# A hybrid decoder step: the first stage in a fixed order on TensorE, VectorE and ScalarE

## The chip, the cores and the metric

The kernel runs on one core of a Trainium2 chip. The core has five engines, each with its own instruction sequence: TensorE (matmuls, in the profile PE, its weight loads PEld), VectorE (DVE), ScalarE (ACT), GpSimd (POOL) and SyncE (SP), which here issues the DMAs. The metric is the device time of one execution in microseconds (us).

## What is computed

The reference is one inference step of a decoder with two layers, for a prompt of 1024 tokens and 8 sample tokens, width 1024. Layer A is a gated delta-rule layer, layer B a sliding-window attention. Only the very beginning of layer A matters here:

```
def gdn_layer(x, conv_buf, s0, norm_g, w_in, conv_w, a_log, dt_bias, o_norm, w_out):
    proj = rmsnorm(x, norm_g) @ w_in
    qkv, gate, a, beta_logit = jnp.split(proj, [CONV_CH, CONV_CH + GDN_V_W, CONV_CH + GDN_V_W + GDN_HEADS], axis=-1)
    qkv, new_buf = causal_conv_silu(qkv, conv_buf, conv_w)
    ...
```

`rmsnorm` divides each token's row by the root of its mean square and multiplies it by a gain. `w_in` has the columns of q, k and v for eight heads of 128, a gate, and 16 columns for a and beta. The q, k and v columns then go through a convolution of four taps along the tokens.

## The kernel before

The 1032 tokens are nine tiles of x: eight of 128 tokens (x0 to x7) and one of 8 sample tokens (x8). They are transposed into three groups of 384, 384 and 264 tokens (`xg[0..2]`), x0 to x2 in the first, x3 to x5 in the second, x6 to x8 in the third. Each group holds a high part, rounded to the format that TensorE reads at full rate, and a low part, the rest.

*One x tile* (loop at L296 to L311). ScalarE squares the row and sums it (L301). VectorE takes the inverse root by nine small operations that each need the one before (`rsqrt`, L121 to L133), and scales the tile by it and by the gain (L304). TensorE transposes it in two halves, four blocks each, into a PSUM buffer (L308, tile name `xps`); ScalarE casts a half into the high part (L310), VectorE subtracts that from PSUM for the low part (L311). The PSUM pool `gen` has two buffers, so a half can be transposed only when the low part of the half before last is done.

*The projections.* `first_proj(gi)` (L279) does three things for one group: the a/b projection of 16 matmuls (tile `psab`), which ScalarE copies into `abT` (L285), and one projection of 24 matmuls each for the k and the q columns of head 0 (tile `pj`), whose results ScalarE copies into the convolution's input `ue` (L215 to L218). The PSUM pool `pj` has two buffers too. The weights come through `load_w`: two DMAs into raw buffers, of which there are two, ScalarE's cast to the high part (L80), VectorE's subtraction to the low part (L81). After the loop over the tiles come the three groups (L320), then the gate projection of head 0 (L323), and a block with raised priority that turns `abT` into decay factors (from L327, tiles `pst`, `psg`, `pss`).

*The taps.* At tile number `CT` = 5 TensorE also transposes the convolution's weights and stored rows (L317, tile `cps`), 24 small transposes, into `cvT`.

*The order of the work.* The first stage is written in the order above, but a scheduler in the compiler decides the order on each engine: an instruction that is ready may go ahead of others that wait. Buffers of one pool are handed out in the order of the program. DMAs are issued on SP in the order of `LO` = "0g12k345q678": x0, the gain, x1, x2, the k weights, x3 to x5, the q weights, x6 to x8, and behind them the a/b weights (L268) and the taps (L274). The nine x tiles share eight buffers. The stage that follows (L542 in the profile) has an order written out by a planner in the kernel, which keeps to it on all engines.

Of the kernel before, what the change touches and what calls it, by code (L numbers as in the profile page):

```python
# [23 lines left out]
NT = 8  # L24
# [32 lines left out]
def hybrid_step(  # L57
# [77 lines left out]
    def rsqrt(*a, **k):  # L135
        for _ in rsq(V, *a, **k):
            pass
# [65 lines left out]

    ues = []

    def conv_open(m):
        ue = uep.tile([P, 1060], F32, tag="ue", name="ue")
        G.memset(ue[:, 0:3], 0.0)
        G.tensor_copy(svw(ue)[:, :, 0:3], cvT[:, m, 0:24].rearrange("p (b i) -> p b i", i=3))
        return ue  # L210

    def conv_evac(ue, m, gi, ps):
        g0, gn = GRP[gi]
# [17 lines left out]
    with tc.tile_pool(name="p2a", reuse_waits="tile", bufs=1) as p2a, \  # L231
# [27 lines left out]
        ws0 = []  # L259
        for o in LO:  # L260
            if o == "g":
                DMA.dma_start(out=gbc, in_=norm_a[0:1, :].broadcast_to([P, D]))
            elif o in "kq":
                ws0.append(load_w(H * P if o == "k" else 0, w_in_a[0]))
            else:
                load_x(int(o))
        wab = p2a.tile([P, KT, 16], F32, name="wab")
        DMA.dma_start(out=wab, in_=w_in_a[0, :, 4096:4112].rearrange("(k p) c -> p k c", p=P))  # L268
        wabp = p2a.tile([P, KT, P], F32R, name="wabp")
        V.tensor_scalar_mul(wabp, ones.unsqueeze(1).broadcast_to([P, KT, P]), 0.0)  # L270
        V.tensor_copy(wabp[:, :, 0:16], wab)
        V.tensor_tensor(out=wabp[:, :, 32:48], in0=wab, in1=wabp[:, :, 0:16].bitcast(F32), op=ALU.subtract)
        cvr = p2a.tile([28, 3072], F32, name="cvr")
        DMA.dma_start(out=cvr[0:24], in_=state_conv[0].rearrange("b i c -> (b i) c"))  # L274
        DMA.dma_start(out=cvr[24:28], in_=conv_w_a[0])
        sel = p2a.tile([64, 16], F32, name="sel")
        V.tensor_tensor(out=sel, in0=ident[:64, 0:16], in1=ident[:64, 32:48], op=ALU.add)
        abT = p2a.tile([64, T], F32, name="abT")

        def first_proj(gi):  # L280
# [5 lines left out]
            for j, w in enumerate(ws0):  # L286
                m = (1 - j) * H
                if gi == 0:
                    ues.append((0, m, 1 - j, conv_open(m)))
                ps = pj.tile([P, 512], F32, tag="pj", name="pj")  # L290
                for _ in proj_group(*w, xg[gi], gn, ps):
                    pass
                conv_evac(ues[j][3], m, gi, ps)

        for t in range(NT + 1):
            n = P if t < NT else NS  # L296
            g, off = divmod(t * P, 384)
            xt = xts[t]
            junk = p1.tile([P, D], BF16, tag="junk", name="junk", bufs=1)
            r = sm.tile([P, 1], F32, tag="r1", name="r1")  # L300
            S.activation(junk[:n], xt[:n], AF.Square, accum_out=r[:n])  # L301
            ri = sm.tile([P, 1], F32, tag="ss", name="ri")
            rsqrt(ri[:n], r[:n], 1, 1.0 / D, EPS, n, tag="b")
            V.scalar_tensor_tensor(out=xt[:n], in0=xt[:n], scalar=ri[:n], in1=gbc[:n], op0=ALU.mult, op1=ALU.mult)  # L304
            for hf in range(2):
                ps = gps("xps").rearrange("p (k t) -> p k t", k=4)
                for k in range(4):
                    PE.transpose(ps[:, k, :n], xt[:n, ts(4 * hf + k, P)], ident[:n, :n])  # L308
                hi = xg[g][:, 0, 4 * hf:4 * hf + 4, off:off + n]
                S.copy(hi, ps[:, :, :n])  # L310
                V.tensor_tensor(out=xg[g][:, 1, 4 * hf:4 * hf + 4, off:off + n], in0=ps[:, :, :n],  # L311
                                in1=hi.bitcast(F32), op=ALU.subtract)
            if t == CT:
                for q in range(2):
                    ps = gps("cps")
                    for j in range(12):
                        PE.transpose(ps[:, j * 28:j * 28 + 28], cvr[:, ts(12 * q + j, P)], ident[:28, :28])  # L317
                    S.copy(cvT[:, 12 * q:12 * q + 12, :].rearrange("p a b -> p (a b)"), ps[:, :12 * 28])
                V.tensor_scalar_mul(cvT[:, :, 24:28], cvT[:, :, 24:28], 0.5)
        for gi in range(3):  # L320
            first_proj(gi)
        hd[0]["og"] = ogs[:, 0]
        wz = load_w(3 * H * P, w_in_a[0])  # L323
        for gi in range(3):
# [1537 lines left out]
```

## Time and profile before

| | |
|---|---|
| runs | 1304.68, 1306.94, 1301.55 us, median 1304.68 |
| profiled execution | 1303.65 us, its span 1302.0 us |
| TensorE busy | 1227.2 us, 94% |
| VectorE, ScalarE, GpSimd busy | 71%, 49%, 22% |
| mean granted TensorE clock | 0.986 of 2.4 GHz |
| chain that ended last | TensorE 70%, VectorE 17%, ScalarE 4%, DMA 4% |

The span runs from the first to the last instruction of the program. An engine is busy while one of its instructions executes; matmuls are pipelined, so that the time of one row in the timeline is longer than the distance to the next. Times in the trace count from the span's start. A granted clock of 0.50 is 1.2 GHz, 1.00 is 2.4 GHz.

### The profile page before, as it was taken

How to read it: one execution, taken by the hardware profiler on the slowest of the kernel's cores; microseconds unless marked ns; L12 is line 12 of the kernel's file. 1: busy time of each engine (PE TensorE's matmuls, PEld its weight loads, DVE VectorE, ACT ScalarE, POOL GpSimd, SP SyncE). 2: the span in 40 equal slices, each digit the busy share in tenths (PEclk: the TensorE clock that was granted, in tenths of full speed). 3: DMA queues.
4: the chain of work that ended last, by engine and by line, in shares of the span. 5: the costliest groups of instructions: out<-in, count | busy, mean ns of one | idle time of the engine just before them, and what ended most of it. 6: DMA issues, size and time to landing. Idle time of an engine off the chain costs nothing.

```text
span 1302.0 us, 24333 instructions
## 1 busy us (share of the span) xinstructions
PE 1227.2 (94%) x8887; PEld 1112.0 (85%) x8887; DVE 926.3 (71%) x2656; ACT 634.8 (49%) x1812; POOL 288.4 (22%) x404
## 2 busy tenths in 40 slices
PE   4999999999999999998999978999989999999998
PEld 3989898989999989888988746888878888988897
DVE  7468988878979897788877358686675677677221
ACT  5236555645455553546453137375565556567100
POOL 1036423424324353253301122120030020000000
PEclk9999999999999999999999989999999999999999
DMA  7021111110221322111256666121030030102322
GB/s 239 1 81 35 36 33 36 37 51 18 68 66 35 98 67 84 36 36 31 61 176 195 200 220 176 34 59 26 1 82 3 1 82 20 33 2 88 117 91 73
DMA packets 131987, 92.03 MB, mean 71 GB/s; under 512 B 33880, under 2 KB 123712, under 8 KB 131808
## 3 DMA queue, kind: packets, MB, share of 16 engines
q1 hardware_dynamic: 131868, 90.48, 23.6%
q8 instruction: 70, 1.15, 0.4%
q14 instruction: 49, 0.40, 0.1%
HBM read 69.28 MB, written 23.25 MB: 71 GB/s over the span
## 4 chain that ended last, share of the span: by engine, by line
PE 70%; DVE 17%; ACT 4%; DMA 4%; issue 3%; POOL 2%; SPq 0%; DVEq 0%; ACTq 0%; POOLq 0%
PE pj L542 24%; PE pj L99 17%; PE ivt L542 4%; DVE co L542 3%; PE sps L99 3%; PE chB L542 3%; PE op L99 2%; PE chA L542 2%; PE ptp L1645 1%; DMA out_dram<-hx 1%; DVE wqkv L81 1%; PE sp L542 1%; PE nps L542 1%; PE tq L1592 1%; PE psab L99 1%
## 5 line engine op out<-in xcount | busy, mean ns | idle before, releaser
L542 PE MATMUL pj<-xg,whi 128*128 128x384 f32 (+1 forms) x1392 | 289.9, 335 | 1.0 <-ACT whi L542 1.0
L542 PEld LDWEIGHTS pj<-xg,whi 128*128 128x128 f32 x1392 | 222.6, 190 | 2.7 <-ACT whi L542 1.2
L99 PE MATMUL pj<-wqkv,ng 128*128 128x384 f32 x768 | 154.6, 346 | 0.0
L542 PE MATMUL pj<-xg,wlo 128*128 128x384 f32 (+1 forms) x696 | 151.9, 335 | 0.0
L542 DVE SCALAR_TENSOR_TENSOR co<-ue,cvT,co 128x528 f32<-128x528 f32 x144 | 134.6, 941 | 16.1 <-ACT co L542 14.5
L99 PEld LDWEIGHTS pj<-wqkv,ng 128*128 128x128 f32 x768 | 133.2, 191 | 5.0 <-issue 4.6
L542 PEld LDWEIGHTS pj<-xg,wlo 128*128 128x128 f32 x696 | 111.8, 189 | 1.4 <-issue 0.7
L92 POOL TENSOR_TENSOR raw<-raw,gains 128x512 f32<-128x512 f32 x40 | 45.8, 1154 | 255.5 <-DMA raw<-in_w_in_b_dram 147.1
L99 PE MATMUL pj<-wob,oh 128*128 128x384 f32 (+1 forms) x576 | 98.1, 325 | 0.0
L99 PEld LDWEIGHTS pj<-wob,oh 128*128 128x128 f32 x576 | 90.7, 191 | 1.8 <-issue 1.5
L542 PE MATMUL pj<-woa,ohl 128*128 128x512 f32 x288 | 76.1, 406 | 0.0
L542 PEld LDWEIGHTS pj<-woa,ohl 128*128 128x128 f32 x288 | 51.7, 188 | 11.6 <-issue 1.5
L542 ACT COPY ue<-pj 128x384 f32<-128x384 f32 (+1 forms) x88 | 31.7, 377 | 53.1 <-PE pj L542 46.1
L1823 DVE TENSOR_TENSOR hx<-hx,pj 128x384 f32<-128x384 f32 (+3 forms) x27 | 13.7, 508 | 60.5 <-PE pj L99 45.9
L542 POOL TENSOR_TENSOR ue<-ue,co 128x528 f32<-128x528 f32 x24 | 33.9, 1412 | 71.1 <-ACT ue L542 71.1
L542 DVE TENSOR_TENSOR wlo<-raw,whi 128x512 fp32r<-128x512 f32 x58 | 43.6, 758 | 7.7 <-ACT whi L542 7.6
L542 ACT ACTIVATE ue<-co 128x528 f32<-128x528 f32 x48 | 30.8, 644 | 29.9 <-DVE co L542 27.7
L542 ACT CAST whi<-raw 128x512 fp32r<-128x512 f32 x58 | 35.8, 619 | 16.8 <-PE pj L542 16.5
L542 POOL TENSOR_TENSOR co<-co,ue 128x528 f32<-128x528 f32 x24 | 39.3, 1636 | 1.3
L99 PE MATMUL op<-pt,vsb 128*64 128x256 f32 x240 | 37.9, 396 | 0.9 <-DVE e L1629 0.8
L1536 ACT ACTIVATE jk<-pj 128x320 f32<-128x320 f32 x32 | 13.9, 435 | 50.4 <-PE pj L99 50.4
L99 PE MATMUL pj<-woa,ohl 128*128 128x512 f32 x96 | 27.7, 442 | 11.2 <-DVE ohl L1420 5.8
(906 smaller groups left out, 2965.9 us busy)
## 6 DMA issues: line engine op xcount, KB each, us to landing
raw<-in_w_in_a_dram SPq DMA_DIRECT2D x64, 256.0 KB
ssm<-in_state_ssm_dram SPq DMA_DIRECT2D x32, 256.0 KB
hD<-hx SPq DMA_DIRECT2D x16, 512.0 KB
raw<-in_w_in_b_dram SPq DMA_DIRECT2D x32, 256.0 KB
xt<-in_x_prompt_dram SPq DMA_DIRECT2D x8, 512.0 KB
out_dram<-ssm SPq DMA_DIRECT2D x16, 256.0 KB
raw<-in_w_out_a_dram SPq DMA_DIRECT2D x16, 256.0 KB
hx<-in_x_prompt_dram SPq DMA_DIRECT2D x8, 512.0 KB
```

Source lines behind the costliest of these rows:

```text
L81: V.tensor_tensor(out=lo, in0=raw, in1=hi.bitcast(F32), op=ALU.subtract)
L92: G.tensor_tensor(out=raw, in0=raw, in1=gain[:, k:k + n].unsqueeze(2).broadcast_to([P, n, c]), op=ALU.mult)
L99: PE.matmul(out, lhsT, rhs, start=start, stop=stop, skip_group_check=True)
L542: op.f(*op.a, **op.k)
L1536: S.activation(jk[:n], src, AF.Square)
L1592: PE.transpose(tq[:, ts(h, P)], qhl[:, h].rearrange("p a d -> p (a d)"), identr)
L1645: PE.transpose(pp[:, ts(h, P)], pr[h // 2][:, h % 2, ts(kt, P)], ident)
L1823: V.tensor_tensor(out=hx[:n, :cn], in0=hx[:n, :cn], in1=ps[:n, :cn], op=ALU.add)
```

## The change

The work of the tiles, from x0 to the second group's first convolution projection, is now written in one block in which TensorE, VectorE and ScalarE keep the written order (`manual_schedule`). The steps of a tile become functions: `square`, `scale`, `turn` (the transposes and both parts, a half at a time). `norm_group` squares two or three tiles, takes their inverse roots in one chain of nine operations on up to three columns, and scales them. `first_proj` is split into `first_ab` and `first_conv`; `weave` lets the next half of a tile be transposed after every four matmuls of a projection (the taps after every ten). SP's order becomes "0g12ak345678q": the a/b weights stand behind x2, the k weights come as one DMA into a buffer of their own, the q weights are loaded inside the block (`second_w`), the taps after the first convolution projection. The convolution inputs are opened (`conv_open`, on GpSimd) at the end. `turn_taps` does what L315 to L319 did. Everything from the gate projection on is as before.

```diff
-LO = "0g12k345q678"
-CT = 5
+LO = "0g12ak345678q"
...
+        wk_raw = p1.tile([P, KT, P], F32, name="wk_raw")
+        wk = [whl.tile([P, KT, P], F32R, tag=f"w{a}", name=f"w{a}") for a in ("hi", "lo")]
+        ws0 = [wk]
...
+            elif o == "a":
+                DMA.dma_start(out=wab, in_=w_in_a[0, :, 4096:4112].rearrange("(k p) c -> p k c", p=P))
+            elif o == "k":
+                DMA.dma_start(out=wk_raw, in_=w_in_a[0][:, H * P:H * P + P].rearrange("(k p) c -> p k c", p=P))
+            elif o != "q":
                 load_x(int(o))
...
+        def turn(t):
+            n = P if t < NT else NS
+            g, off = divmod(t * P, 384)
+            for hf in range(2):
+                ps = gps("xps").rearrange("p (k t) -> p k t", k=4)
+                for k in range(4):
+                    PE.transpose(ps[:, k, :n], xts[t][:n, ts(4 * hf + k, P)], ident[:n, :n])
+                hi = xg[g][:, 0, 4 * hf:4 * hf + 4, off:off + n]
+                S.copy(hi, ps[:, :, :n])
+                V.tensor_tensor(out=xg[g][:, 1, 4 * hf:4 * hf + 4, off:off + n], in0=ps[:, :, :n],
+                                in1=hi.bitcast(F32), op=ALU.subtract)
+                yield
+
+        def norm_group(tiles):
+
+            n_ = len(tiles)
+            r = sm.tile([P, 3], F32, tag="r1", name="r1")
+            if NT in tiles:
+                V.memset(r, 1.0)
+            ri = sm.tile([P, 3], F32, tag="ss", name="ri")
+            for i, t in enumerate(tiles):
+                square(t, r[:, i:i + 1])
+            rsqrt(ri[:, :n_], r[:, :n_], n_, 1.0 / D, EPS, tag="b")
+            for i, t in enumerate(tiles):
+                scale(t, ri[:, i:i + 1])
...
+        def first_conv(gi, j):
+            if gi == 0:
+                ues.append((0, (1 - j) * H, 1 - j, uep.tile([P, 1060], F32, tag="ue", name="ue")))
+            ps = pj.tile([P, 512], F32, tag="pj", name="pj")
+            yield from proj_group(*ws0[j], xg[gi], GRP[gi][1], ps)
+            conv_evac(ues[j][3], (1 - j) * H, gi, ps)
+
+        def weave(a_, b_, n):
+
+            for i, _ in enumerate(a_):
+                if i % n == n - 1:
+                    next(b_, None)
+            for _ in b_:
+                pass
...
+        def second_w():
+            ws0.append(load_w(0, w_in_a[0]))
+            yield
...
+        with tc.manual_schedule(engines={mybir.EngineType.PE, mybir.EngineType.DVE, mybir.EngineType.Activation}):
+            norm_group([0])
+            r = sm.tile([P, 3], F32, tag="r1", name="r1")
+            for i in range(2):
+                square(1 + i, r[:, i:i + 1])
+            for _ in turns([0]):
+                pass
+            ri = sm.tile([P, 3], F32, tag="ss", name="ri")
+            rsqrt(ri[:, :2], r[:, :2], 2, 1.0 / D, EPS, tag="b")
+            for i in range(2):
+                scale(1 + i, ri[:, i:i + 1])
+            V.tensor_copy(wabp[:, :, 0:16], wab)
+            V.tensor_tensor(out=wabp[:, :, 32:48], in0=wab, in1=wabp[:, :, 0:16].bitcast(F32), op=ALU.subtract)
+            for _ in turns([1, 2]):
+                pass
+            for a in range(2):
+                split(wk[0][:, ts(a, 4)], wk[1][:, ts(a, 4)], wk_raw[:, ts(a, 4)])
+            norm_group([3, 4, 5])
+            first_ab(0)
+            weave(first_conv(0, 0), seq(turns([3, 4]), second_w(), turns([5])), 4)
+            DMA.dma_start(out=cvr[0:24], in_=state_conv[0].rearrange("b i c -> (b i) c"))
+            DMA.dma_start(out=cvr[24:28], in_=conv_w_a[0])
+            norm_group([6, 7, 8])
+            weave(first_conv(0, 1), turns([6, 7, 8]), 4)
+            first_ab(1)
+            weave(first_conv(1, 0), turn_taps(), 10)
+        for _ in first_conv(1, 1):
+            pass
+        first_ab(2)
+        for j in range(2):
+            for _ in first_conv(2, j):
+                pass
+        for j in range(2):
+            conv_open(ues[j][3], ues[j][1])
         hd[0]["og"] = ogs[:, 0]
         wz = load_w(3 * H * P, w_in_a[0])
```

## Rows read from the trace of the kernel before

**Rows 1.** The page, part 1: busy us of TensorE, share, instructions.

```profile
PE 1227.2 (94%) x8887; PEld 1112.0 (85%) x8887; DVE 926.3 (71%) x2656; ACT 634.8 (49%) x1812; POOL 288.4 (22%) x404
```

**Rows 2.** Busy time of each engine by stretch, up to the next stage.

```profile
core 0: us, PE busy (x) PEld busy (x) DVE busy (x) ACT busy (x) POOL busy (x), PEclk, DMA share, GB/s
0.00:27.00 27.00, 7.47 (x33) 6.33 (x33) 19.24 (x83) 16.34 (x29) 4.46 (x19) 1.00 0.85 254
27.00:47.00 20.00, 20.00 (x134) 18.79 (x132) 14.90 (x46) 8.47 (x19) 0.34 (x2) 1.00 0.12 47
47.00:81.40 34.40, 34.27 (x224) 33.11 (x223) 10.61 (x45) 7.33 (x19) 0.25 (x1) 1.00 0.15 47
```

**Rows 3.** Who TensorE waited for, 0 to 100 us.

```profile
PE xps L308 <- DVE xt L304: 13.5, 2, 11.2
PE xps L308 <- DVE xg L311: 6.0, 2, 3.8
PE dps L542 <- POOL gm L542: 1.3, 1, 1.3
PE pj L542 <- ACT whi L542: 1.0, 1, 1.0
```

**Rows 4.** Timeline (start us, us, engine, line, operation), x0: square, root's first step, scaling.

```profile
6.90 1.06 ACT L301 ACTIVATE junk<-xt 128x1024 bf16<-128x1024 f32 x1 [2.83 <-DMA xt<-in_x_prompt_dram]
...
8.08 0.15 DVE L121 TENSOR_SCALAR rs_x<-r 128x1 f32<-128x1 f32 x1 [2.64 <-ACT junk L301]
...
9.81 1.28 DVE L304 SCALAR_TENSOR_TENSOR xt<-xt,ri,gbc 128x1024 f32<-128x1024 f32 x1
```

**Rows 5.** Timeline, ScalarE and VectorE: x2's square, casts, low parts.

```profile
11.37 1.06 ACT L301 ACTIVATE junk<-xt 128x1024 bf16<-128x1024 f32 x1 [0.16 <-DMA xt<-in_x_prompt_dram]
...
12.43 0.60 ACT L80 CAST whi<-raw 128x512 fp32r<-128x512 f32 x1
...
12.94 0.57 ACT L310 CAST xg<-xps 128x512 fp32r<-128x512 f32 x1
...
20.45 1.28 DVE L311 TENSOR_TENSOR xg<-xps,xg 128x512 fp32r<-128x512 f32 x2
```

**Rows 6.** Timeline, TensorE: the first matmuls of the a/b projection.

```profile
27.00 4.10 PE L99 MATMUL psab<-xg,wabp 128*128 128x384 f32 x12
```

**Rows 7.** Chain that ended last, 36 to 52 us: start us, us, what.

```profile
37.97 1.60 PE cps L317 x24
...
40.82 2.12 PE pj L99 x12
42.94 0.44 PE xps L308 x4
...
46.65 0.77 PE pst L99 x6
47.42 3.01 PE psab L99 x16
```

**Rows 8.** Timeline, VectorE: two steps of interleaved roots.

```profile
23.57 0.15 DVE L132 SCALAR_TENSOR_TENSOR rs_u<-rs_u 128x1 f32<-128x1 f32 x1
23.63 0.15 DVE L128 TENSOR_TENSOR rs_u<-rs_u,ri 128x1 f32<-128x1 f32 x1
```

**Rows 9.** Timeline, VectorE: second operation on the a/b weights.

```profile
26.39 0.28 DVE L272 TENSOR_TENSOR wabp<-wab,wabp 128x128 fp32r<-128x128 f32 x1
```

**Rows 10.** Timeline, ScalarE: the first a/b result leaves PSUM.

```profile
32.72 0.47 ACT L285 COPY abT<-psab 64x384 f32<-64x384 f32 x1
```

**Rows 11.** Two waits elsewhere, and the granted clock (PEclk) behind them.

```profile
486.79 0.66 PE L542 MATMUL ktp<-ident,ktok 128*128 128x128 f32 x4 [2.18 <-DVE ktok L542]
757.12 3.78 PE L99 MATMUL pj<-woa,ohl 128*128 128x512 f32 x8 [5.78 <-DVE ohl L1420]
...
488.30:491.60 3.30, 3.30 (x15) 3.30 (x14) 3.09 (x10) 1.57 (x4) 0.82 (x2) 0.50 0.00 0
757.10:760.90 3.80, 3.78 (x8) 2.48 (x8) 0.30 (x1) 0.00 (x0) 3.51 (x5) 0.50 0.95 276
```

More of the change, by code (lines that the diff above doesn't have):

```diff
@@ L204, in hybrid_step, with conv_open @@
     ues = []
-    def conv_open(m):
-        ue = uep.tile([P, 1060], F32, tag="ue", name="ue")
+    def conv_open(ue, m):
         G.memset(ue[:, 0:3], 0.0)
         G.tensor_copy(svw(ue)[:, :, 0:3], cvT[:, m, 0:24].rearrange("p (b i) -> p b i", i=3))
-        return ue
     def conv_evac(ue, m, gi, ps):
@@ L257, in load_x @@
             xts.append(xt)
-        ws0 = []
+        wab = p2a.tile([P, KT, 16], F32, name="wab")
+        wk_raw = p1.tile([P, KT, P], F32, name="wk_raw")
+        wk = [whl.tile([P, KT, P], F32R, tag=f"w{a}", name=f"w{a}") for a in ("hi", "lo")]
+        ws0 = [wk]
+        wabp = p2a.tile([P, KT, P], F32R, name="wabp")
+        V.tensor_scalar_mul(wabp, ones.unsqueeze(1).broadcast_to([P, KT, P]), 0.0)
+        sel = p2a.tile([64, 16], F32, name="sel")
+        V.tensor_tensor(out=sel, in0=ident[:64, 0:16], in1=ident[:64, 32:48], op=ALU.add)
         for o in LO:
@@ L275, in hybrid_step, with square, scale @@
-        DMA.dma_start(out=cvr[24:28], in_=conv_w_a[0])
-        sel = p2a.tile([64, 16], F32, name="sel")
-        V.tensor_tensor(out=sel, in0=ident[:64, 0:16], in1=ident[:64, 32:48], op=ALU.add)
         abT = p2a.tile([64, T], F32, name="abT")
-        def first_proj(gi):
+        def square(t, r):
+            n = P if t < NT else NS
+            junk = p1.tile([P, D], BF16, tag="junk", name="junk", bufs=1)
+            S.activation(junk[:n], xts[t][:n], AF.Square, accum_out=r[:n])
+        def scale(t, ri):
+            n = P if t < NT else NS
+            xt = xts[t]
+            V.scalar_tensor_tensor(out=xt[:n], in0=xt[:n], scalar=ri[:n], in1=gbc[:n], op0=ALU.mult, op1=ALU.mult)
@@ new lines, in turn @@
+        def turn(t):
+            n = P if t < NT else NS
+            g, off = divmod(t * P, 384)
[8 more added lines that the diff above has]
+                yield
@@ new lines, in norm_group, with turns @@
+        def norm_group(tiles):
[9 more added lines that the diff above has]
+                scale(t, ri[:, i:i + 1])
+        def turns(tiles):
+            for t in tiles:
+                yield from turn(t)
@@ L281, in first_proj, with first_ab @@
+        def first_ab(gi):
             g0, gn = GRP[gi]
@@ L285, in first_proj @@
             S.copy(abT[:, g0:g0 + gn], ps[:64, :gn])
[L286 to L319, printed above, removed]
@@ L320, in hybrid_step @@
-        for gi in range(3):
-            first_proj(gi)
+        def first_conv(gi, j):
[10 more added lines that the diff above has]
+                pass
@@ new lines, in turn_taps @@
+        def turn_taps():
+            for q in range(2):
+                ps = gps("cps")
+                for j in range(12):
+                    PE.transpose(ps[:, j * 28:j * 28 + 28], cvr[:, ts(12 * q + j, P)], ident[:28, :28])
+                S.copy(cvT[:, 12 * q:12 * q + 12, :].rearrange("p a b -> p (a b)"), ps[:, :12 * 28])
+                yield
+            V.tensor_scalar_mul(cvT[:, :, 24:28], cvT[:, :, 24:28], 0.5)
+        def second_w():
+            ws0.append(load_w(0, w_in_a[0]))
+            yield
@@ new lines, in seq @@
+        def seq(*gs):
+            for g_ in gs:
+                yield from g_
+        with tc.manual_schedule(engines={mybir.EngineType.PE, mybir.EngineType.DVE, mybir.EngineType.Activation}):
[24 more added lines that the diff above has]
+            weave(first_conv(1, 0), turn_taps(), 10)
```

10 lines of the change are left out of this document (removed).

## The prediction

> **What bounds the kernel now.** I read the page first: TensorE is busy 94% of the span [rows 1], so time is won or lost where it stands idle. The busy times by stretch say where: 7.5 us of work in the first 27 us, then 20.0 of 20.0 and 34.3 of 34.4 up to the next stage at 81.4 [rows 2]. The waits of TensorE name what it stood for in those 27 us: 13.5 us for VectorE's scaled x tiles, 6.0 us for VectorE's low parts, which free the two PSUM buffers of the transposes [rows 3]. So the first stage is a load and VectorE problem up to 27 us, and a pure TensorE problem after it. A change of order here can win at most what lies ahead of 27 us. It can also lose, by any wait that it puts after 27 us, because nothing there is slack.
>
> **The change, part by part.** I follow the new order instruction by instruction, on the time axis of the trace of before. One engine takes its instructions in the order in which the code now writes them.
>
> *Prices.* A squared row costs ScalarE 1.06 us [rows 4]. One inverse root is a chain of nine dependent VectorE operations, from 8.08 to 9.81: 1.75 us with its start. The scaling takes 1.28 us, 1.21 to the next one [rows 4]. ScalarE's casts follow each other by 0.5 us, 0.6 us long; VectorE's low parts by 0.61 us, 0.68 long [rows 5]. Four transposes take 0.44 us and a 384-column matmul 0.177 at the higher clock level; at the lower one, at which the first twelve matmuls ran, 0.34 each (the clock column reads 1.00 there; twice the spacing says 1.2 GHz), 0.32 from start to start [rows 6, 7].
>
> *Batched inverse roots.* Nine chains of nine become four. This looks like 45 operations saved, but in before the chains of different tiles are interleaved: operations of two chains start 0.06 us apart [rows 8], where those of one chain start 0.19 apart (1.75 by nine). Eight interleaved chains of nine at 0.06 and the lone first one (1.75) are 6.1 us of VectorE; four serial chains are 7.0. So nothing is won by the count; the steps below take each new chain at its 1.75. The Trainium skill ("VectorE: DVE Perf Modes", "The DRAIN you can't avoid" and "Rules for kernel authors") says that the next operation does not issue until the pipe is empty, so that only the count matters; by it 45 times 0.19, or 8.6 us of VectorE, would be saved. The trace does not agree: 0.06 us between starts of operations 0.15 us long.
>
> *Start of the first projection.* Loads of x0, the gain, x1 and x2 keep their places, so x2 is still there at 11.4 [rows 5]. Its square ends at 12.4; the casts of x0 at 13.3 to 13.9; x0's second low part frees VectorE at 14.5; roots of x1 and x2 to 16.2; x1 is scaled at 17.5, x2 at 18.7; the two operations on the a/b weights, the longer 0.28 [rows 9], take it to 19.3. The transposes, still at the lower level (0.23 each: 7.47 us for 33 in [rows 2]), the cast and the low part of x1's first half end at 20.0 and free a buffer for x2, whose second cast lands at 22.7. The a/b projection starts at 22.0 instead of 27.0: 5.0 us won. Eight transposes of x3, which before did ahead of 27, are still to come (0.9 lost), and all 16 matmuls may run at the lower level, where 11 did (0.7 lost).
>
> *The second group.* ScalarE has behind that cast two casts of the k weight (to 23.65), then the squares of x3 to x5 (3.2, to 26.9). VectorE's root takes 1.75 (28.7), the first scaling 1.28: x3's transposes start at 30.1. TensorE has finished the a/b projection (16 x 0.32 from 22.0: 27.1) and the four matmuls written ahead of them (27.9): 2.2 us of new waiting. From there to x5's last transposes 20 matmuls (3.5), 24 transposes (2.6), six changes between matmuls and transposes (an estimated 0.1 each, 0.6) and one wait of 0.5, since x3's low part, which frees the buffer for x4, is now behind the scalings of x4 and x5: TensorE is at 37.5.
>
> *The third group* decides. The squares of x6 to x8 are written after everything of the first convolution projection, so ScalarE reaches them only behind x5's last cast, at 38.3. Three squares: 41.5. Roots: 43.3. First scaling: 44.6. Transposes of x6: 44.8. TensorE has only four matmuls (37.5 to 38.2) before them in its own order: 6.6 us of waiting. In before it was never idle here [rows 2]. Behind the waiting transposes stand 20 matmuls, the a/b projection and all that follows; nothing may pass. Even later projections left to the scheduler can't, for the PSUM ring is served in program order: before had the a/b result at 33.2, but its high-priority pst took its turn in the other ring at 46.65, after the last transposes [rows 7, 10]. From 44.8: 20 matmuls 3.5, 24 transposes 2.4 (x8's are short), changes 0.6, a wait of 0.5, 16 matmuls 2.8: the second a/b projection ends at 54.5.
>
> *Comparison.* In before it ends at 50.4 with the tap transposes (1.60) and the first pst group (0.77) already done [rows 7]; without these, 48.1. New minus old: 6.5 us. As a sum: -5.0 + 0.9 + 0.7 + 2.2 + 0.5 + 6.6 + 0.5 = 6.4.
>
> *The clock.* Some 1.5 us after a wait of 2.2 us elsewhere in this kernel TensorE ran 3.3 us at granted 0.50, the level of 1.2 GHz; after one of 5.8 us it came back at 0.50 and did 3.8 us of work at it [rows 11]. After the new waits I take 3.4 us at half rate in the second group (0.6 on the path, the rest lies under VectorE) and 4 us in the third (1.4): 2.0 us. Below, nothing; above, about 4.5 if the third group stays low to its end.
>
> *Loads.* On SP's queue the a/b weights and one whole transfer of the k weights now stand ahead of x3; x3 to x7 no longer stand behind the q weights' raw buffers; only x8 still waits, for x0's buffer, free at 13. At the 254 GB/s of [rows 2] x3 (1.1 MB behind x2) is in by 16, x5 by 20, x7 by 24; the squares ask for them at 23.7, 25.8 and 39.3. I cost the loads at nothing: ScalarE's order covers them by 6 us or more. Were ScalarE ready for x3 right behind x2's square, at 12.4, x3 would be 3.4 us late.
>
> *After the fixed part* the code is as before, and TensorE has 34.3 us of work in 34.4 [rows 2]: what is late at its start is late at its end, and the next stage hangs on that.
>
> Sum: 6.5 + 2.0 = 8.5 us on the profiled execution's 1303.65 (span 1302.0 and 1.65 around it): 1312.2. The median of the runs, 1304.68, is 1.0 above that execution. I predict 1312.
>
> **Rivals.**
> *Not slower: the long wait does not arise.* Place: ScalarE and VectorE between x5's last cast and x6's scaling. If the squares of x6 to x8 are run ahead (x6 is loaded by 24) and their roots and scalings slip under the first convolution projection, the third group loses its 6.6 and its share of the clock, and the sum is -5.0 + 0.9 + 0.7, or -3.4, if the other new waits go with it, and -3.4 + 3.2 + 0.6 = 0.4 if they stay: 1300 to 1304. For it: such work was hidden in before, where VectorE had 5 us free of 20 from 27 on [rows 2]. Against it: the code order, which I take as binding. It decides whether x6's transposes start within about 2 us of the fourth matmul.
> *Partly swallowed later.* At the start of the next stage TensorE waits 1.0 us for a weight cast and 1.3 for a decay [rows 3]; if VectorE got ahead there, and no clock were lost, the sum would be 6.5 - 2.3, 1308. Against: both hang on the end of this stage.
> *The clock stays low.* Between waits the third group is a sparse mix, and the a/b projection after it may also run at 0.50: 54.5 becomes 57.4 to 58.8, that is 1315 to 1318. The skill ("TensorE: Matmul & The Clock Gate", "HAM oscillation") has an array re-throttled by each round's wait, with every round starting cold, which is this case; [rows 11] show it after two waits.
>
> **How the numbers follow.** Forecast 0.58, its own range 1308 to 1316; not slower 0.18; swallowed 0.10; clock 0.10; something unseen 0.04. A measurement tells about 0.5%, 6.5 us, from no change: slower means above 1311.2. Of the forecast 0.40 lies above it and 0.18 below, plus the clock's 0.10 and 0.02 unseen: slower 0.52. Same: 0.18 + 0.10 and 0.13 of the not-slower case: 0.41. Faster needs more than any term here gives (of the 19.5 us idle in [rows 2], 11.2 pass before x0 is scaled [rows 3]): 0.07. The range runs from inside the not-slower case to the top of the clock's: 1300 to 1318.
>
> **What would show it.** In the new profile: the first a/b matmul near 22; x3's transposes near 30, x6's near 45 with an idle time of 5 to 7 us ahead of them, released by the scaling; VectorE and ScalarE in single file in front of it; granted clock at 0.50 after it; the second a/b projection ending near 55 to 57. I am wrong if no wait of TensorE after 30 is over 2 us, or if the stage ends as early as before despite it.

## The result and the profile after

The changed kernel is slower: median 1316.55 us (1311.15 to 1319.87) against 1301.55 us (1297.54 to 1306.94) of the kernel before on the same chip, seven runs each. The ratio is 1.0105, with a 95% interval of 1.0082 to 1.0128; that is 13.7 us, between 10.7 and 16.7. The profiled execution took 1319.66 us, its span 1318.0.

The busy times by stretch of the changed kernel, cut as in [rows 2], with a fourth stretch up to the start of the next stage, which is now at 95.4 us and was at 82.5:

```profile
0.00:27.00 27.00, 9.96 (x44) 8.53 (x44) 14.71 (x44) 12.49 (x21) 4.46 (x19) 1.00 0.82 269
27.00:47.00 20.00, 8.61 (x49) 8.15 (x50) 13.48 (x32) 8.88 (x18) 0.00 (x0) 0.83 0.23 79
47.00:81.40 34.40, 32.98 (x223) 30.95 (x222) 13.81 (x51) 9.85 (x25) 0.57 (x3) 0.95 0.01 1
81.40:95.40 14.00, 13.06 (x72) 12.84 (x72) 2.73 (x5) 2.28 (x6) 0.00 (x0) 0.89 0.14 39
```

TensorE does 2.5 us more in the first 27 us (9.96 for 7.47) and then stands idle for 11.4 of 20.0 us, where in [rows 2] it was never idle. The waits of TensorE up to 100 us, as in [rows 3], name the cause: VectorE's low parts have all but gone from the list (6.0 us before, 0.5 now), and the scaled tiles cost 27.9 us for 13.5.

```profile
PE xps L292 <- DVE xt L284: 27.9, 4, 11.3
PE pj L609 <- ACT whi L609: 1.0, 1, 1.0
PE psg L98 <- DVE gf L435: 0.9, 1, 0.9
PE xps L292 <- DVE xg L295: 0.5, 1, 0.5
PE pj L98 <- ACT whi L79: 0.5, 1, 0.5
```

The timeline of the changed kernel (start us, us, engine, line, operation, in brackets the idle time ahead and what ended it), TensorE first and then what ScalarE and VectorE do in the long wait:

```profile
21.98 3.59 PE L98 MATMUL psab<-xg,wabp 128*128 128x384 f32 x16
25.40 0.86 PE L98 MATMUL pj<-xg,whi 128*128 128x384 f32 x4
30.48 1.09 PE L292 MATMUL xps<-ident,xt 128*128 128x128 f32 x4 [4.21 <-DVE xt L284]
...
37.93 0.95 PE L98 MATMUL pj<-xg,whi 128*128 128x384 f32 x4
46.80 1.08 PE L292 MATMUL xps<-ident,xt 128*128 128x128 f32 x4 [7.92 <-DVE xt L284]
...
54.76 3.09 PE L98 MATMUL psab<-xg,wabp 128*128 128x384 f32 x16
57.68 1.58 PE L98 MATMUL pj<-xg,whi 128*128 128x384 f32 x8
...
38.25 0.49 ACT L212 COPY ue<-pj 128x384 f32<-128x384 f32 x1
38.62 0.60 ACT L294 CAST xg<-xps 128x512 fp32r<-128x512 f32 x1
40.05 1.06 ACT L279 ACTIVATE junk<-xt 128x1024 bf16<-128x1024 f32 x1 [0.82 <-ACT xg L294]
...
39.90 0.06 DVE L304 MEMSET r<- 128x3 f32 x1
43.59 0.17 DVE L120 TENSOR_SCALAR rs_x<-r 128x3 f32<-128x3 f32 x1 [3.62 <-ACT junk L279]
```

The first a/b projection starts at 21.98. x3's transposes come after 4.21 us of waiting, x6's after 7.92. In front of x6's everything is in single file: x5's last cast at 38.62, the memset of the sums at 39.90 behind x5's last low part, the first square at 40.05, the roots at 43.59. The second a/b projection is over at 57.7; before, without taps and `pst`, that point was at 48.1 [rows 7]. So 9.6 us of the delay stand there.

Another 3.4 us come up to the next stage. They sit at the gate projection of head 0, in code that the change did not touch. First the kernel before, then the changed one, timelines around the cast of the gate weights and the next stage's first matmuls (L542, L609):

```profile
65.98 1.15 ACT L80 CAST whi<-raw 128x512 fp32r<-128x512 f32 x2
...
69.77 0.51 PE L99 MATMUL pj<-xg,wlo 128*128 128x384 f32 x2
70.41 0.41 PE L99 MATMUL psg<-gf,mle 128*128 128x64 f32 x2
...
82.47 1.68 PE L542 MATMUL pj<-xg,whi 128*128 128x384 f32 x8 [0.99 <-ACT whi L542]
```

```profile
80.44 0.33 ACT L447 ACTIVATE eG<-psg 128x192 f32<-128x192 f32 x1 [1.05 <-PE psg L98]
80.66 1.13 ACT L79 CAST whi<-raw 128x512 fp32r<-128x512 f32 x2
...
79.55 0.41 PE L98 MATMUL psg<-gf,mle 128*128 128x64 f32 x2 [0.91 <-DVE gf L435]
81.33 2.93 PE L98 MATMUL pj<-xg,whi 128*128 128x384 f32 x8 [0.51 <-ACT whi L79]
95.44 1.68 PE L609 MATMUL pj<-xg,whi 128*128 128x384 f32 x8 [0.99 <-ACT whi L609]
```

Before, ScalarE cast the gate weights ahead of the decay factors, and the gate's first matmuls filled the time in which the decay was worked out. Now the cast stands behind `eG`, so TensorE waits for the decay (0.91) and then for the cast (0.51), and the eight matmuls behind that run at half clock (2.93 us for eight; granted 0.50 from 81.1 to 84.6). From the next stage on the matched matmuls of the two traces stay 12.1 to 13.0 us apart up to 540 us; what is added later (17 us at the end of these two traces) comes with falls of the granted clock, which lie differently in each execution. The 13.0 us at the start of the next stage and the 13.7 us of the ratio agree.

### The profile page after: what moved, and what is told of

It is laid out like the page before. It is cut to its first block, busy times and chain, and to the rows that moved or that the text cites. A ratio compares the mean times of both kernels' runs of the same rounds, so it can differ in the third digit from the quotient of the medians.

```text
span 1318.0 us, 24284 instructions
## 1 busy us (share of the span) xinstructions
PE 1234.9 (94%) x8887; PEld 1118.3 (85%) x8887; DVE 925.3 (70%) x2612; ACT 634.6 (48%) x1812; POOL 286.6 (22%) x404
## 3 DMA queue, kind: packets, MB, share of 16 engines
q1 hardware_dynamic: 131852, 90.48, 23.1%
## 4 chain that ended last, share of the span: by engine, by line
PE 68%; DVE 18%; ACT 4%; issue 3%; DMA 2%; POOL 2%; SPq 0%; DVEq 0%; ACTq 0%; POOLq 0%
PE pj L609 23%; PE pj L98 17%; PE ivt L609 4%; DVE co L609 3%; PE sps L98 3%; PE chB L609 3%; PE op L98 2%; PE chA L609 2%; PE ptp L1712 1%; DVE wqkv L80 1%; DMA out_dram<-hx 1%; PE tq L1659 1%; PE sp L609 1%; DVE f L609 1%; DVE fu L609 1%
## 5 line engine op out<-in xcount | busy, mean ns | idle before, releaser
L609 PE MATMUL pj<-xg,whi 128*128 128x384 f32 (+1 forms) x1392 | 289.3, 335 | 1.0 <-ACT whi L609 1.0
L609 PEld LDWEIGHTS pj<-xg,whi 128*128 128x128 f32 x1392 | 222.0, 190 | 2.7 <-ACT whi L609 1.2
L609 PE MATMUL pj<-xg,wlo 128*128 128x384 f32 (+1 forms) x696 | 153.0, 336 | 0.0
L609 DVE SCALAR_TENSOR_TENSOR co<-ue,cvT,co 128x528 f32<-128x528 f32 x144 | 134.2, 938 | 7.4 <-ACT co L609 5.8
L609 PEld LDWEIGHTS pj<-xg,wlo 128*128 128x128 f32 x696 | 112.8, 191 | 1.4 <-issue 0.7
L609 PE MATMUL pj<-woa,ohl 128*128 128x512 f32 x288 | 76.1, 406 | 0.0
L609 PEld LDWEIGHTS pj<-woa,ohl 128*128 128x128 f32 x288 | 51.8, 188 | 11.5 <-issue 1.5
L609 ACT COPY ue<-pj 128x384 f32<-128x384 f32 (+1 forms) x88 | 31.7, 377 | 52.8 <-PE pj L609 45.8
L1890 DVE TENSOR_TENSOR hx<-hx,pj 128x384 f32<-128x384 f32 (+3 forms) x27 | 13.7, 508 | 59.3 <-PE pj L98 47.7
L609 POOL TENSOR_TENSOR ue<-ue,co 128x528 f32<-128x528 f32 x24 | 33.9, 1411 | 72.3 <-ACT ue L609 72.3
L609 DVE TENSOR_TENSOR wlo<-raw,whi 128x512 fp32r<-128x512 f32 x58 | 43.6, 757 | 7.7 <-ACT whi L609 7.6
L609 ACT ACTIVATE ue<-co 128x528 f32<-128x528 f32 x48 | 30.8, 644 | 29.8 <-DVE co L609 27.6
L609 ACT CAST whi<-raw 128x512 fp32r<-128x512 f32 x58 | 35.8, 619 | 17.0 <-PE pj L609 16.5
L292 PE MATMUL xps<-ident,xt 128*128 128x128 f32 (+1 forms) x72 | 14.3, 348 | 28.4 <-DVE xt L284 27.9
L609 POOL TENSOR_TENSOR co<-co,ue 128x528 f32<-128x528 f32 x24 | 38.9, 1622 | 1.3
```

Of the source, the lines that this page charges most:

```text
L292: PE.transpose(ps[:, k, :n], xts[t][:n, ts(4 * hf + k, P)], ident[:n, :n])
L609: op.f(*op.a, **op.k)
L1890: V.tensor_tensor(out=hx[:n, :cn], in0=hx[:n, :cn], in1=ps[:n, :cn], op=ALU.add)
```

## The experiments

The ratios are to the kernel before, timed on the same chip each time. Two times of the first stage say more than the medians: the second a/b projection and the start of the next stage (82.47 before, 95.44 after).

**The scheduler decides again.** Only the fixed order goes.

```diff
-        with tc.manual_schedule(engines={mybir.EngineType.PE, mybir.EngineType.DVE, mybir.EngineType.Activation}):
+        with ExitStack():
```

> The changed kernel without the fixed order: the scheduler again chooses the order of TensorE, VectorE and ScalarE; the loads, the grouped inverse roots and the weaving in the program text stay. Changed kernel now: TensorE idle 4.2 us ahead of x3's transposes and 7.9 us ahead of x6's, first matmul of the next stage at 95.4 (before: 82.5). Order theory (the written order puts the squares of x6 to x8 behind everything of the first convolution projection, and that makes the waits and the low clock): no wait of TensorE over 2 us after 30 us, gate weights cast before the gate's matmuls need them, next stage at 80 to 84, time 12 to 16 us below the changed kernel's, within 0.3% of before. Rival (grouped roots, one k transfer and the woven text cost by themselves): next stage at 90 or later, time at most 5 us below the changed kernel's.

Measured: 1298.9 us, ratio 0.9959 (0.9943 to 0.9975). All waits of TensorE from 27 us on, and the next stage's first matmul:

```profile
PE dps L609 <- POOL gm L609: 1.5, 2, 1.3
PE pj L609 <- ACT whi L609: 1.0, 1, 1.0
...
79.57 1.68 PE L609 MATMUL pj<-xg,whi 128*128 128x384 f32 x8 [0.98 <-ACT whi L609]
```

Both long waits are gone, and so is the delay ahead of the next stage; the next stage is 15.9 us earlier than in the changed kernel and 2.9 earlier than before. The time is 0.4% below before, a little more than expected. So the loss is the written order, and none of it is in grouped roots, loads or woven text.

**A fixed order for x0 to x2 only.** The block ends ahead of the squares of x3 to x5.

```diff
+        with ExitStack():
             norm_group([3, 4, 5])
             first_ab(0)
```

> The changed kernel, whose fixed order ends behind the k weights' low parts: x0 to x2 in the written order, everything from the squares of x3 on is left to the scheduler. Theory (the harm lies in the order written for the second and third group and in what it does to the gate weights' place; that of the first group costs nothing): first a/b matmul at 22.0, no wait of TensorE over 1.5 us between 27 us and the next stage, which starts at 78.5 to 82 for 95.4, time 12 to 17 us below the changed kernel. Rival (a fixed order for the first group alone already makes the stage late): next stage at 85 or later.

Measured: 1298.41 us, ratio 0.9970 (0.9941 to 0.9999); first a/b matmul at 22.10, no wait over 1.4 us from 27 us on, next stage at 78.73.

```profile
78.73 1.68 PE L610 MATMUL pj<-xg,whi 128*128 128x384 f32 x8 [0.99 <-ACT whi L610]
```

A fixed order does no harm where it is written for the first group.

**Another fixed order.** Squares of x3 to x5 in ScalarE's idle time ahead of 19 us, grouped roots cut up between low parts, each scaling just ahead of its tile's transposes. The squares of x6 to x8 come ahead too, and the gate weights have a buffer of their own, as in the run on them below; the lines shown have neither.

```diff
+            for i in range(3):
+                square(3 + i, r3[:, i:i + 1])
...
+            for n, _ in zip((1, 3, 1, 4), turns([1, 2])):
+                steps(g3, n)
+            scale(3, ri3[:, 0:1])
...
+                for _ in turn(4):
+                    steps(g6, 2)
+                    yield
...
+                scale(6, ri6[:, 0:1])
```

> A fixed order again, but another one: the squares of x3 to x5 in ScalarE's idle time between 14 and 19 us, those of x6 to x8 behind the k weights' casts and between the casts of x3 and x4, the grouped roots cut up and put between low parts, each scaling just ahead of its tile's transposes; gate weights as in e6. Order theory: first a/b projection at 22 to 23.5, no idle time of TensorE over 2 us from 27 us to the next stage, which starts at 79 to 84; time 1298 to 1305, that is 11 to 18 us below the changed kernel. Rival (a fixed order by itself, or the grouped roots, costs): next stage at 88 or later.

Measured: 1298.13 us, ratio 0.9977 (0.9956 to 0.9998). One wait over 2 us was left, 3.0 us ahead of x6's transposes at 38.16, and the next stage starts at 81.33. The expectation was none over 2 us. So it is not fixing that costs, but this order; mine is no better than the scheduler's.

**Squares of x6 to x8 ahead, two forms.** In the first the memset of their sums stands behind the scalings of x3 to x5 on VectorE.

```diff
             norm_group([3, 4, 5])
+            r678 = sm.tile([P, 3], F32, tag="r1", name="r678")
+            V.memset(r678, 1.0)
+            for i in range(3):
+                square(6 + i, r678[:, i:i + 1])
...
-            norm_group([6, 7, 8])
+            ri6 = sm.tile([P, 3], F32, tag="ss", name="ri")
+            rsqrt(ri6, r678, 3, 1.0 / D, EPS, tag="b")
+            for i in range(3):
+                scale(6 + i, ri6[:, i:i + 1])
```

> Fixed order kept; only the three squares of x6 to x8, with the memset of their sums, are written ahead, behind those of x3 to x5. Roots, scalings and transposes stay where they are. Order theory: x6's transposes start 3.5 to 4.3 us earlier than in the changed kernel (46.8), at 42.5 to 43.3, the idle time ahead of them falls from 7.9 to about 4, the next stage starts 3.5 to 6 us earlier than 95.4 (the upper end if the clock stays high), the time is 3 to 6 us lower. Rival (the wait is set by the loads of x6 to x8, or the next stage by something other than this wait): x6's transposes or the next stage move by less than 1 us.

Measured: 1316.93 us, ratio 1.0102 (1.0076 to 1.0129), nothing won; the next stage starts at 98.16, 2.7 us later than in the changed kernel. Its timeline:

```profile
32.65 0.06 DVE L374 MEMSET r<- 128x3 f32 x1
32.79 1.06 ACT L279 ACTIVATE junk<-xt 128x1024 bf16<-128x1024 f32 x1 [5.58 <-issue]
37.91 1.11 PE L292 MATMUL xps<-ident,xt 128*128 128x128 f32 x4 [3.60 <-DVE xg L295]
49.52 0.63 PE L292 MATMUL xps<-ident,xt 128*128 128x128 f32 x4 [4.20 <-DVE xt L284]
```

The memset of 0.06 us ran at 32.65, behind three scalings; the squares waited 5.58 us for it, and x3's casts behind the squares, so a new wait of 3.60 us ahead of x4's transposes took what the one ahead of x6 gave back (4.20 for 7.92). This was my edit, not the load: in the next run the same squares ran at 27.2 to 30.5 without a wait. The Trainium skill ("Perfetto Trace Analysis", "Tensor Engine Instruction (MATMUL, LD_WEIGHTS)") calls ScalarE, VectorE and GpSimd strict FIFO; this row shows what that costs.

The second form writes the memset ahead of the roots of x3 to x5.

> As the run with the squares of x6 to x8 ahead, whose squares stood 5.6 us behind a memset that VectorE reached only after the scalings of x3 to x5; here that memset is written ahead of the roots of x3 to x5. Order theory: squares of x6 to x8 end near 30.7, no new wait ahead of x4's transposes, x6's roots follow x5's last low part (about 39.9), so x6's transposes start at 42.5 to 43.5 with about 4 us idle ahead of them (changed kernel: 46.8 and 7.9), next stage 3 to 6 us earlier than 95.4, time 2 to 6 us lower. Rival (the wait of TensorE only moves, as it did in that run): sum of TensorE's waits between 27 and 60 us stays at 11 to 13 us, next stage within 1.5 us of 95.4.

Measured: 1314.72 us, ratio 1.0100 (1.0065 to 1.0136).

```profile
44.05 1.08 PE L292 MATMUL xps<-ident,xt 128*128 128x128 f32 x4 [4.19 <-DVE xt L284]
...
93.45 1.68 PE L616 MATMUL pj<-xg,whi 128*128 128x384 f32 x8 [0.98 <-ACT whi L616]
```

The wait falls to 4.19 us and x6 comes 2.75 us earlier, less than the 3.5 expected, since the second group now runs 1.0 us later at half clock (x5's last transposes end at 38.9). The next stage is 2.0 us earlier: the theory's direction, but under its 3 to 6, and the time can't be told from the changed kernel's. TensorE's waits between 27 and 78 us: 12.1 us after, 12.0 with the late memset, 8.8 here, which is outside the rival's 11 to 13. The squares' place is 3.3 us of the waits. Of the rest, 4.2 us stand ahead of x6, where roots and first scaling still come behind x5's last low part, and 4.6 ahead of x3, where this run changed nothing.

**The gate weights in their own buffer.** It is the one that the k weights have left.

```diff
-        wk_raw = p1.tile([P, KT, P], F32, name="wk_raw")
+        wk_raw = p1.tile([P, KT, P], F32, tag="w_raw", name="wk_raw", bufs=1)
...
+            wz_raw = p1.tile([P, KT, P], F32, tag="w_raw", name="wz_raw", bufs=1)
+            DMA.dma_start(out=wz_raw, in_=w_in_a[0][:, 3 * H * P:3 * H * P + P].rearrange("(k p) c -> p k c", p=P))
...
-        wz = load_w(3 * H * P, w_in_a[0])
+        wz = [whl.tile([P, KT, P], F32R, tag=f"w{a}", name=f"wz{a}") for a in ("hi", "lo")]
+        for a in range(2):
+            split(wz[0][:, ts(a, 4)], wz[1][:, ts(a, 4)], wz_raw[:, ts(a, 4)])
```

> Changed kernel with one thing altered: the gate's raw weights get the buffer that the k weights have left and are loaded right behind the third group, so that their transfer no longer stands behind that of the cache; fixed order kept. Theory of the tail (of the 13.0 us by which the next stage is late, 9.6 stand at the end of the second a/b projection and about 3.3 come between it and the next stage, because the gate weights' cast moved behind the decay chain on ScalarE, 80.7 for 66.0): first a/b and x6 as in the changed kernel (22.0, 46.8), no idle time over 0.5 us ahead of the gate's matmuls, next stage at 91.5 to 93, time 2 to 4 us lower. Rival (the tail is only the low clock and the decay chain that came late with the rest): next stage at 94.5 to 96.

Measured: 1312.68 us, ratio 1.0070 (1.0048 to 1.0092).

```profile
75.38 1.15 ACT L79 CAST wzhi<-wz_raw 128x512 fp32r<-128x512 f32 x2
...
77.76 1.57 PE L98 MATMUL pj<-xg,wzhi 128*128 128x384 f32 x8
...
91.85 1.33 PE L613 MATMUL pj<-xg,whi 128*128 128x384 f32 x6 [0.98 <-ACT whi L613]
```

The cast is back ahead of the decay chain, the two waits are gone, and the next stage starts 3.6 us earlier, 0.75 of which already stood at the second a/b projection. So what is added behind the second a/b projection is worth 2.8 us, the half clock at 81.1 included, which this run does not have. It is the cast's place and not its transfer: in the changed kernel hardly a byte moved from 58 to 81.4 us (DMA share 0.00, 1 GB/s), so that the weights had long been there. Whether the buffer or the place of the load in the text moved the cast was not separated.

**Filling the long wait.** 40 matmuls whose result the next one overwrites.

```diff
+            if (gi, j) == (0, 1):
+                for _ in range(40):
+                    mm(ps[:, :384], ws0[j][0][:, 0, :], xg[0][:, 0, 0, :384])
             yield from proj_group(*ws0[j], xg[gi], GRP[gi][1], ps)
```

> The changed kernel with 40 extra 384-column matmuls (7.1 us at the higher clock) ahead of the second first-group projection, into the bank that its first matmul overwrites: they stand in the wait ahead of x6's transposes and leave everything else. Theory (the wait itself is set by ScalarE and VectorE, and the low clock from 43.6 to 50.4 is a consequence of TensorE standing idle): x6's transposes still at 46.3 to 47.3, granted clock 1.00 from 36 to 60, second a/b projection ends 1 to 2 us earlier than 57.7, next stage 1 to 2 us earlier than 95.4. Rival (the clock falls whatever TensorE does there): granted 0.50 behind 43 us as before, second a/b projection within 0.5 us of 57.7 or later.

Measured: 1313.26 us, ratio 1.0093 (1.0058 to 1.0128). Timeline, then stretches with the granted clock (third column from the end), the last line that of the changed kernel:

```profile
38.21 8.01 PE L98 MATMUL pj<-xg,whi 128*128 128x384 f32 x44
47.11 0.63 PE L292 MATMUL xps<-ident,xt 128*128 128x128 f32 x4 [0.89 <-DVE xt L284]
...
43.60:50.40 6.80, 5.50 (x35) 4.86 (x35) 6.20 (x14) 1.43 (x4) 0.00 (x0) 1.00 0.18 77
64.80:68.20 3.40, 3.40 (x13) 3.40 (x12) 1.55 (x3) 1.22 (x2) 0.00 (x0) 0.50 0.01 2
...
43.60:50.40 6.80, 3.60 (x14) 3.54 (x15) 5.72 (x13) 0.93 (x2) 0.00 (x0) 0.50 0.19 79
```

x6's transposes come 0.3 us later, no earlier, so the wait is ScalarE's and VectorE's, and the clock stays at 1.00 from 43.6 to 50.4, where the changed kernel had 0.50: there the idle time made it fall. The four other runs that kept a wait of over 4 us ahead of x6 had a fall there too (late memset, early memset, gate weights, roots one by one in the fixed order, at 50.5, 42.4, 42.8 and 44.0); the one with 3.0 us of waiting had none. From x6's transposes to the end of the second a/b projection it takes 9.8 us for 10.9: the low clock cost 1.0 us. That it cost no more because x7 and x8 were still being scaled in it is likely, but not shown. The second a/b projection is over 0.7 us earlier, for the 1 to 2 expected. But the gain did not reach the next stage (96.15): the clock fell at 64.8, in steady work, where it had not in the changed kernel. So the expectation missed in both times.

**Roots one by one.** First in the fixed order, then without it; the edit is the same.

```diff
-            rsqrt(ri[:, :n_], r[:, :n_], n_, 1.0 / D, EPS, tag="b")
+            for i, t in enumerate(tiles):
+                rsqrt(ri[:, i:i + 1], r[:, i:i + 1], 1, 1.0 / D, EPS, tag="b")
```

> The changed kernel with its fixed order, but in each group one root chain per tile, one behind the other, before the scalings (the pair x1, x2 stays grouped). The chains can't interleave here, since the order is fixed, but the first can start when its own tile's square is done, while the squares still run (pitch 1.18 us). Theory: the last of three roots ends 3 x 1.75 us behind the first square, 1.1 to 1.4 us later than the grouped root, in both groups: x3's transposes at 31.5 to 32.0 (changed kernel: 30.5), x6's at 48.5 to 49.8 (46.8), next stage 2 to 3 us later than 95.4. So grouping is worth about 1.2 us a group in a fixed order, where without one it was worth nothing. Rival (each extra operation counts in full, 18 times 0.19 us a group): x6's transposes at 53 or later.

> The kernel without the fixed order, with one root chain of nine per tile in place of the grouped ones; nothing else. Theory of the forecast (chains of several tiles interleave at 0.06 us from start to start, so grouping wins nothing): next stage within 1 us of the 79.6 of the run without the fixed order, time within 0.2% of its 1298.9. Rival (only the count of VectorE's operations matters: 45 more at 0.19 us are 8.6 us): next stage 3 us later or more, time 3 to 9 us higher.

Measured with the fixed order, a single execution (1316.71 us, too few for a ratio): x3's transposes at 31.14, x6's at 49.61, next stage at 98.74, 3.3 us later than with groups. x3 is 0.7 us later, less than the 1.0 to 1.5 expected; x6 2.8, of which 2.1 were there when x5's transposes ended (40.05 for 37.93, at half clock until 37.2). So in a fixed order grouping is worth 0.7 us a group, and the rest is the clock. Without the fixed order: 1298.86 us, ratio 0.9974 (0.9953 to 0.9995), next stage at 79.76 for 79.57. Chains interleave again, as these two rows of its VectorE show:

```profile
20.23 0.15 DVE L124 TENSOR_SCALAR ri<-rs_x 128x1 int32<-128x1 int32 x1
20.29 0.15 DVE L129 TENSOR_TENSOR rs_u<-rs_x,ri 128x1 f32<-128x1 f32 x1
```

The equal end flatters the theory: up to 50 us this run is 1.7 us later than the grouped one (first a/b matmul 23.09 for 22.48, clock high from 27.3 for 24.2), and is level only because the grouped one had a fall of the clock at 51.5. So the end time decides little here; VectorE's busy time in the first 50 us does (third pair of numbers), first grouped, then one by one:

```profile
0.00:50.00 50.00, 33.14 (x206) 30.39 (x207) 31.92 (x83) 25.21 (x47) 4.80 (x21) 1.00 0.49 156
0.00:50.00 50.00, 32.58 (x188) 29.84 (x188) 33.13 (x119) 25.24 (x47) 4.82 (x21) 1.00 0.49 156
```

The edit leaves the pair x1, x2 grouped, so that it adds 36 operations and not the 45 of the expectation. They cost VectorE 1.2 us, where a count at 0.19 us each gives 6.8. So grouping is worth little, at most 1.7 us. The Trainium skill says "Minimize op *count*, not sems" of chained operations ("VectorE: DVE Perf Modes", "Rules for kernel authors"); a price by the count is not what this run shows. The section that the prediction names beside it, "The DRAIN you can't avoid" of the Trainium skill, has an exception that the prediction left out, "A next op that is not held starts earlier", and the two rows of interleaved chains, 0.06 us apart at 0.15 us each, show such a start.

**The loads alone.** The kernel before, no fixed order, no grouping: first with the whole new order of loads, then with the a/b weights alone moved ahead.

```diff
-LO = "0g12k345q678"
+LO = "0g12ak345678q"
...
+            elif o == "a":
+                DMA.dma_start(out=wab, in_=w_in_a[0, :, 4096:4112].rearrange("(k p) c -> p k c", p=P))
```

> The kernel before with only the order of the loads changed as in the change: the a/b weights ahead of the k weights, the q weights behind x8. No fixed order, roots one by one. It asks where the 4 to 5 us come from by which the kernel without the fixed order is faster than before. Theory (the a/b projection can start when x0 to x2 are there, and x3 to x8 no longer stand behind the q weights' raw buffers): first a/b matmul at 22 to 24 for 27.0, next stage at 78.5 to 81 for 82.5, time 2 to 6 us below before. Rival (the loads are hidden anyway; the gain comes from the woven text and grouped roots): first a/b matmul at 26 or later, next stage within 1 us of 82.5, time within 0.1% of before.

Measured: 1295.99 us, ratio 0.9966 (0.9940 to 0.9992); first a/b matmul at 22.50, next stage at 78.38. The second run has `LO = "0g12ak345q678"`.

> The kernel before with one load moved: the a/b weights ahead of the k weights. The q weights stay ahead of x6 to x8. It splits the gain of the run with the new order of all loads (first a/b matmul 22.5 for 27.0, next stage 78.4 for 82.5). Theory (the first a/b projection stood behind its own weights, whose second operation ran at 26.4 on VectorE): first a/b matmul at 22.0 to 23.5, next stage at 78 to 80, time 2 to 6 us below before. Rival (it is x3 to x8 coming ahead of the q weights): first a/b matmul at 25 or later, or next stage at 81 or later.

Measured: 1297.3 us, ratio 0.9968 (0.9945 to 0.9991). Its timeline:

```profile
12.86 0.29 DVE L273 TENSOR_TENSOR wabp<-wab,wabp 128x128 fp32r<-128x128 f32 x1
22.45 4.00 PE L99 MATMUL psab<-xg,wabp 128*128 128x384 f32 x16
78.03 1.68 PE L543 MATMUL pj<-xg,whi 128*128 128x384 f32 x8 [0.98 <-ACT whi L543]
```

In before the same VectorE operation ran at 26.39 [rows 9], and the a/b projection right behind it at 27.00 [rows 6]: it stood behind its own weights. Moving one small load ahead brings the next stage to 78.0, 4.4 us earlier: all that the change has to give, in one line.

**Keeping TensorE busy from the start.** The new loads, and 58 matmuls of ones ahead of the first transposes.

```diff
+        psw = pj.tile([P, 512], F32, tag="pj", name="psw")
+        def warm(n_):
+            for _ in range(n_):
+                mm(psw[:, :P], ones, ones)
+        warm(40)
         for t in range(NT + 1):
...
+            if t < 2:
+                warm(10 - 2 * t)
```

> The kernel before with the order of the loads of the change, as in the earlier run, plus 58 matmuls of ones by ones (128 columns, result not used) on TensorE: 40 ahead of x0's transposes, 12 and 6 ahead of those of x1 and x2, where TensorE stood idle. Theory (the clock is low up to 25.2 because TensorE stands idle before, and its transposes lie between VectorE's operations): granted clock 1.00 before 20 us, transposes of x1 and x2 at 0.11 us each for 0.23, first a/b matmul at 20.8 to 22.2 for 22.5 and all 16 at 0.18, next stage at 75.5 to 77.5 for 78.4. Rival (VectorE sets the pace there, and the second a/b projection is paced by it too): next stage within 0.5 us of 78.4, whatever the clock.

Measured: 1294.39 us, ratio 0.9955 (0.9929 to 0.9981), the interval overlapping that of the loads alone.

```profile
1.28 11.18 PE L99 MATMUL psw<-ones 128*128 128x128 f32 x80 [1.28 <-DVE ones L110]
22.66 1.67 PE L99 MATMUL psab<-xg,wabp 128*128 128x384 f32 x8 [0.69 <-ACT xg L318]
78.77 1.68 PE L552 MATMUL pj<-xg,whi 128*128 128x384 f32 x8 [0.98 <-ACT whi L552]
...
25.00:46.40 21.40, 21.40 (x154) 19.94 (x152) 16.13 (x48) 9.77 (x22) 0.34 (x2) 1.00 0.22 74
46.40:49.80 3.40, 3.40 (x12) 3.36 (x12) 0.00 (x0) 0.00 (x0) 0.00 (x0) 0.50 0.00 0
```

Each of these matmuls shows as two records. The clock is high from 5.5 us on (these matmuls start 0.21 us apart before, 0.11 behind), but the first a/b projection starts at 22.66 for 22.50: ScalarE's casts and VectorE pace that part, as the rival has it. Its matmuls run faster (1.1 us won around 30 us), which the fall at 46.4 takes back. Next stage +0.4.

Both kernels are beaten by every version without the changed kernel's order of the second and third group; their ratios, 0.9955 to 0.9977, can't be told apart, and two of the intervals reach to 0.9998 and 0.9999.

## Why the prediction was right, and where it fell short

Right were the direction, the place and the mechanism of the two waits; the forecast of 8.5 us was too small beside 13.0 in the trace and 13.7 in the runs.

| step | predicted | measured |
|---|---|---|
| first a/b projection starts | 22.0 | 21.98 |
| x3's transposes | 30.1 | 30.48 |
| wait ahead of them | 2.2 | 4.21 |
| TensorE through with x5's transposes | 37.5 | 37.93 |
| squares of x6 to x8 from, roots | 38.3, 43.3 (end) | 40.05, 45.3 (end) |
| x6's transposes, wait | 44.8, 6.6 | 46.80, 7.92 |
| second a/b projection over, with the clock | 56.5 | 57.7 |
| from there to the next stage | 0 added | 3.4 added |

*Start and second group.* The 5.0 us won are real, and the a/b weights alone win them. The wait ahead of x3 was 2.0 us longer than forecast. 1.6 of these come from the clock, which rose at 23.1 (the matmuls start 0.32 us apart before, 0.18 behind) where I had the lower level up to 27: TensorE was done at 26.3 for 27.9. The other 0.4 is the scaling that came later, behind three squares at the price given below.

*Third group.* The mechanism is as forecast, 2.0 us later. 0.9 of them stand at x5's last cast (39.2 for 38.3): 0.4 in TensorE, at the low clock (0.6 in my clock term), and the rest in the copy of the first projection's result (L212, 0.49), which ScalarE takes ahead of that cast. 0.8 is the memset of the sums, which I left out: it holds the first square back behind x5's last low part. 0.3 is the price of a square: 1.18 us from start to start with the reading of its sum, where I took the 1.06 of its first row.

*The clock.* 3.4 us (from 29.9) and 6.8 us (from 43.6) at 0.50 came where I put them, the second for 4 us forecast; it cost 1.0 us by the filled wait, for 1.4. The rival "stays low" is out for the changed kernel: the 16 matmuls of the second a/b projection took 3.09 us, the higher level. The page it leaned on ("TensorE: Matmul & The Clock Gate" of the Trainium skill, "HAM oscillation") describes a fall after each wait, and that the trace shows; it rose again before this work was through.

*The step that failed* is the one on the time after the fixed part: "the code is as before", and so "what is late at its start is late at its end". The code was as before, the order was not: the gate weights' cast changed places with the decay chain, for 2.8 us by experiment and 3.4 in the traces (what the 0.6 between them is stays open). With it and the 1.2 us by which the second a/b projection ended later than forecast, 8.5 becomes 13.1.

*Rivals.* "Not slower" named its price rightly: without the two waits it gave -3.4 us, and the three runs without this order of the later groups have -2.9 (scheduler), -3.7 (first group fixed) and -1.1 (my order) at the next stage. Its condition did not hold, since the order is binding. The scheduler's run had a fall of the clock of some 1.5 us in it, so that the fit is no closer than that. "Partly swallowed" is out: the waits at the next stage remained, and 3.4 us were added ahead of it.

*Luck, and two sums.* The measured 1316.55 lies above the forecast's own range, 1308 to 1316, and in the 1315 to 1318 of "stays low", which the trace rules out; the time alone could not have told them apart. Those 1315 to 1318 don't come out of that rival's own steps: 57.4 to 58.8 for 54.5 adds 2.9 to 4.3 us to the 6.5, with the second group's 0.6 at most 11.4, so 1313 to 1316. The range's upper end, 1318, was taken from there. It also helped that the kernel before had a median of 1301.55 where the prediction started from 1304.68: the ratio of 1.0105 on that is 1318.4. "Slower" itself stood at 0.52, little better than even. A smaller slip: the steps of the second group from 30.1 add up to 37.3, not 37.5.

## What to carry to other kernels

A fixed order must be checked where one group ends and the next begins: squares, roots, scalings and transposes of a group in a row leave the bottleneck engine with nothing, and a 0.06 us memset placed behind long work is as hard a wait as any. Look first for the one load that the first use stands behind: moving it gave here all that the large change could give. And an automatic scheduler may reorder untouched code behind a change, as it did here with the gate weights' cast; read one stage further than the diff.

## What the runs showed of the hardware

The granted clock fell also without any wait: in the run kept busy from the start TensorE worked 21.40 of 21.40 us at 1.00 and then had 3.4 us at 0.50 at 46.4, and the run left to the scheduler had the same at 51.5, the filled one at 64.8, while the kernel before with the new loads had none there. Each cost 1.5 to 1.7 us, by how far the matmuls behind it moved against those of a run without it. I know no cause for their places; differences of 1 to 2 us in the first stage are no larger than one such fall, and I did not read them from medians.

Kept busy from the start, TensorE had the higher clock from 5.5 us on, for 25.2 with the new loads alone. That won nothing at the next stage (78.77 for 78.38): VectorE and ScalarE set the pace up to the first a/b projection, and a fall took back the 1.1 us won behind it.
